# A hybrid decoder layer: how rows of tokens reach the experts, where norm weights are applied, and how roots are taken

## The chip, the core and the metric

The kernel runs on one core of a Trainium2 chip. A core has TensorE (PE in the profile; its weight loads are PEld), VectorE (DVE), ScalarE (ACT), GpSimd (POOL) and SyncE (SP), 16 DMA engines, SBUF and PSUM. Time is device microseconds of one launch; it is the median of several executions, and the profile is of one more.

## What is computed

One decoder layer on x of 1024 tokens by 1024 features, in float32. Cut to the parts that the change touches:

```python
def rms_norm(x, g):
    return x * rsqrt(mean(x * x, -1) + 1e-6) * g

h = rms_norm(x, attn_norm_g)
x = x + parallel_mixer(h)              # sparse and latent attention, both gated
x = x + memory_cross_attention(rms_norm(x, mem_x_norm_g), mem)
h = rms_norm(x, moe_norm_g)
x = x + hierarchical_moe(h)

def hierarchical_moe(h):               # 4 groups of 4 experts, top 2 in the best group
    for e in range(16):
        act = silu(h @ w_gate[e]) * (h @ w_up[e])        # 1024 -> 256
        y = y + combine[:, e] * (act @ w_down[e])        # 256 -> 1024
```

The mixer takes RMS norms of heads, too: of queries and keys of both attentions. Every one of them needs an inverse square root per token and head.

## The kernel before

**Stages.** `prep` norms x, projects it and builds keys and values (0 to about 145 us), scores the sparse attention's index, then runs gate projections (`gates`) on TensorE with two generators beside them: `queries`, which norms and rotates the queries of both attentions, and `topk`, which finds the 256th largest score of each row by 32 counting passes on VectorE and ACT (L1176, L1186). `attention` and the branch products follow, then `merge`: the output projection, memory attention and the router, pipelined by 128-token blocks through the class `Memory`; then `moe`. All products use a pair of float32r tiles, hi (ACT) and lo (the residue, on VectorE or GpSimd), and three matmuls (`mm3`, L522 to L524). The order of the instructions on each engine is set by a planner that simulates the program; the kernel adds only some orderings (`issue_after`).

**Roots.** `rsqrt` (L526 to L540) works on a tile of 128 rows and 1 to 17 columns: an add of eps (L533), a shift and a subtraction on the bits (L534, L535), and three Newton rounds of three instructions (L537 to L539), all on VectorE. It is called 15 times in the projections (11 columns), 12 times in `queries` (17), twice for the memory's keys (2 and 8), four times in `Memory.B` (8, without eps) and eight times in `Memory.F` (1).

**Norm weights of rows.** `Memory.E` adds the memory attention's output to x and sums squares; `F` (L465 to L477) takes the root, copies it to y (L469), scales x by y on ACT in two halves (L473) and multiplies by `moe_norm_g` on GpSimd in four pieces of 256 columns (L477), which also permutes each piece: feature 8i + c of a piece goes to place 32c + i. `G` finishes the router's logits; the class `Route` then ranks the experts in many small VectorE steps, and GpSimd scatters whole rows with their weights to a table in DRAM, `d_xs` (L197), sorted by expert. The permutation is made so that 32x32 transposes of the rows give the layout that the expert weights have, eight consecutive features per partition.

**Experts.** Each expert has a fixed room of rows (`ROOM`: 256, 256, 224, 224, 192, 192, 160, 160, five of 128, three of 96; 2592 in all). Big and small rooms alternate (`ORDER_`). The first 128 rows of experts 0 and 1 are read early, before the last rows are routed. `rows_of` reads n rows in four DMAs, one for each quarter of the features (L1646), as 1 KB packets into `xg` laid out in groups of 32 tokens; then the weights and token numbers, a few bytes per row (`emore`, L1652), which GpSimd turns into `ewt` and `etok` (L1654 to L1659). VectorE transposes each group (L1668) into `xT`, and ACT and VectorE split that into `eT` hi and lo (L1671, L1672). `gate_up` loads gate and up weights in halves of four chunks, 1 MB, into two buffers (`gu_raw`, L1689) and splits them (L1690 ACT, L1691 VectorE); `down` does so for the down weights (L1699, L1701 ACT, L1702 GpSimd). `first_big` and `first_small` make the activations, with rows or weights as the moving operand; `second` multiplies by the down weights, scales on ACT (L1722), and adds the result to the output in DRAM by an indirect DMA (L1708).

In the loop the first half of expert i+1's gate and up weights and then its rows are asked for just ahead of expert i's first product, the other half behind it. SyncE issues all loads in order; a load whose buffer is not free holds those behind it.

Of the kernel before, what the change touches and what calls it, by code (L numbers as in the profile page):

```python
# [267 lines left out]
class Memory:  # L268
# [196 lines left out]
    def F(u, t):  # L465

        K, nc = u.K, u.K.nc
        y = u.d['y', t] = u.ap.tile([128, 1], F32, name="my2", bufs=3)
        nc.vector.tensor_copy(y, K.rsqrt(u.d.pop(('ms2', t)), (128, 1)))  # L469
        for h in range(2):  # L470
            m = slice(h * 512, h * 512 + 512)
            xn = u.ap.tile([128, 512], F32, name="mxn", bufs=2)
            nc.scalar.activation(xn, u.x[:, t, m], AF.Copy, scale=y)  # L473
            for a in range(2):
                c, f = slice(a * 256, a * 256 + 256), slice(h * 512 + a * 256, h * 512 + a * 256 + 256)
                nat = lambda v: v.rearrange("p (i c) -> p i c", c=8)
                nc.gpsimd.tensor_mul(u.x[:, t, f].rearrange("p (c i) -> p i c", c=8), nat(xn[:, c]), nat(u.g_o[:, f]))  # L477
# [14 lines left out]
class Hybrid:  # L492
# [33 lines left out]
    def rsqrt(self, v, shape, eps=True):  # L526
        nc, n = self.nc, shape[-1]
        s = self.sm.tile([128, 17], I32, name="rq_s")
        y = self.sm.tile([128, 17], F32, name="rq_y")
        t = self.sm.tile([128, 17], F32, name="rq_t")  # L530
        s, y, t = s[:, :n], y[:, :n], t[:, :n]
# [98 lines left out]
    def consts(self):  # L630
# [5 lines left out]
        nc.vector.tensor_scalar(self.ident, jp, 0.0, None, op0=OP.is_equal)  # L636
        self.identb = ac.tile([128, 128], BF16, name="identb")
# [980 lines left out]
    def moe(self, route):  # L1618
# [20 lines left out]
        def rows_of(n, ex, exf, r, xg, xT, eT, early=False):  # L1639
# [3 lines left out]
            loads, last_load = [], None  # L1643
# [4 lines left out]
            more, wt, tok = (rt.tile([128, *sh], dt, name=nm, bufs=4) for nm, sh, dt in (("emore", (2, 4), F32), ("ewt", (2, 2), F32), ("etok", (2,), I32)))  # L1648
            for b in range(0, n, 128):
                m, b_ = min(128, n - b), b // 128  # L1650
                mo, w = more[0:m, b_], wt[0:m, b_]
                loads.append(nc.sync.dma_start(mo, table[at, r + b:r + b + m, D:D + 4].rearrange("o p f -> (o p) f")))  # L1652
# [7 lines left out]
            for q in loads:  # L1660
                for p in route.puts:
                    if early and p in route.late:
                        tc.declare_no_dep(q.ins, p.ins, reason="rows of a later block")
                    else:
                        tc.add_manual_dep(q.ins, p.ins.name, mybir.DependencyInfo(mybir.DependencyClass.Sync, mybir.DependencyReason.DATA), reason="rows of the table")
            with tc.issue_after(route.last_ix.ins) if early else nullcontext():
                for g in range(n // 32):
# [261 lines left out]
```

## Time and profile before

| What | us |
|---|---|
| median of 3 executions | 1431.34 (1428.15 to 1440.17) |
| the profiled execution's own time | 1433.15 |
| its span in the profile | 1431.3 |
| busy: PE, DVE, ACT, POOL | 1247.2, 976.1, 807.8, 550.6 |
| mean granted clock of TensorE | 0.937 |

The span runs from the first to the last instruction, so the execution has 1.85 us around it. Times in rows are counted from the start of the span. [...]

### The profile page before, as it was taken

Reading aid. Unit: us, or ns where it says so; the run is one execution under the profiler, and the core shown is the slowest. Engines: PE = TensorE matmul, PEld = TensorE weight load, DVE = VectorE, ACT = ScalarE, POOL = GpSimd, SP = SyncE. Lnnn points to the kernel's source line nnn. Section 1 sums busy time; section 2 is a strip of 40 time slices with the busy share of each in tenths; the row PEclk is TensorE's granted clock in tenths of the full one; section 3 lists DMA queues with packets and bytes.
Section 4 is the critical chain, followed back from the end, with each engine's and each line's share of the span. In section 5 each row is a group of like instructions: output and inputs, shape, how many; then the busy total and the mean of one; then the engine's idle time right before and its main releaser. Section 6 shows DMA issues by size and latency. Waiting matters only on the chain.

```text
span 1431.3 us, 20967 instructions
## 1 busy us (share of the span) xinstructions
PE 1247.2 (87%) x6684; PEld 1039.1 (73%) x6685; DVE 976.1 (68%) x2248; ACT 807.8 (56%) x1659; POOL 550.6 (38%) x676
## 2 busy tenths in 40 slices
PE   4779799998888999999998999999997478888993
PEld 4768688776666778888687787788986356777762
DVE  6785775989999757778887566232368977565660
ACT  5453554787663378888998421033454346556662
POOL 4575200425543111221343221211326555577673
PEclk9889899999999999999999999999997789999897
DMA  6555102535343454436321234621103679899973
GB/s 196 154 155 151 46 19 73 154 110 149 112 135 125 145 154 149 144 142 199 89 88 53 72 112 139 211 69 38 59 31 121 248 213 286 244 274 278 258 227 69
DMA packets 154154, 203.58 MB, mean 142 GB/s; under 512 B 70576, under 2 KB 102192, under 8 KB 154032
## 3 DMA queue, kind: packets, MB, share of 16 engines
q1 hardware_dynamic: 145440, 173.22, 39.6%
q0 software_dynamic: 7440, 24.71, 6.4%
q10 hardware_dynamic: 1152, 4.19, 0.7%
q8 instruction: 55, 0.90, 0.3%
q14 instruction: 67, 0.55, 0.1%
HBM read 134.61 MB, written 69.70 MB: 143 GB/s over the span
## 4 chain that ended last, share of the span: by engine, by line
PE 33%; DVE 22%; DMA 13%; ACT 10%; issue 8%; SPq 2%; POOL 2%; ACTq 0%; DVEq 0%; POOLq 0%
PE acc L522 3%; PE acc L523 3%; PE acc L524 3%; DMA xg<-d_xs 3%; PE s L522 2%; PE s L524 2%; PE s L523 2%; DVE ik_lo L1176 2%; DMA out_dram<-ey,etok 2%; DMA gu_raw<-in_moe_w_up_dram 2%; DVE ik_hi L1176 2%; PE s L919 2%; PE tp L1342 2%; DMA gu_raw<-in_moe_w_gate_dram 2%; DVE gu_lo L1691 1%
## 5 line engine op out<-in xcount | busy, mean ns | idle before, releaser
L514 POOL TENSOR_TENSOR wl<-wr,wh 128x512 fp32r<-128x512 f32 (+2 forms) x94 | 119.4, 1288 | 211.1 <-ACT wh L513 167.6
L510 DVE TENSOR_TENSOR PT_lo<-tp,PT_hi 128x512 fp32r<-128x512 f32 x152 | 102.0, 685 | 28.9 <-ACT PT_hi L509 27.4
L522 PE MATMUL s<-hT_hi,wh 128*128 128x512 f32 x256 | 102.5, 400 | 4.2 <-ACT s L1047 4.2
L1186 ACT ACTIVATE tk_junka<-sc,tk_b 128x512 bf16<-128x512 f32 (+2 forms) x96 | 79.4, 827 | 42.4 <-DVE tk_b L1183 27.3
L524 PE MATMUL s<-hT_hi,wl 128*128 128x512 f32 x256 | 101.5, 402 | 1.5 <-POOL wl L514 1.5
L523 PE MATMUL s<-hT_lo,wh 128*128 128x512 f32 x256 | 102.3, 400 | 0.0
L513 ACT ACTIVATE wh<-wr 128x512 fp32r<-128x512 f32 (+2 forms) x94 | 55.7, 610 | 82.2 <-PE acc L524 28.0
L509 ACT ACTIVATE PT_hi<-tp 128x512 fp32r<-128x512 f32 x152 | 86.9, 594 | 20.1 <-PE tp L1342 8.6
L522 PE MATMUL acc<-wh,hT_hi 128*128 128x512 f32 (+2 forms) x240 | 87.2, 365 | 8.8 <-ACT hT_hi L509 4.4
L1702 POOL TENSOR_TENSOR dn_lo<-dn_raw,dn_hi 128x1024 fp32r<-128x1024 f32 x32 | 83.2, 2625 | 16.7 <-ACT dn_hi L1701 16.4
L524 PE MATMUL acc<-wh,hT_lo 128*128 128x512 f32 (+2 forms) x240 | 88.5, 369 | 1.1 <-DVE hT_lo L510 1.1
L1691 DVE TENSOR_TENSOR gu_lo<-gu_raw,gu_hi 128x1024 fp32r<-128x1024 f32 x60 | 77.1, 1310 | 17.7 <-ACT gu_hi L1690 17.7
L523 PE MATMUL acc<-wl,hT_hi 128*128 128x512 f32 (+2 forms) x240 | 87.5, 364 | 0.9 <-POOL wl L514 0.9
L1690 ACT ACTIVATE gu_hi<-gu_raw 128x1024 fp32r<-128x1024 f32 x60 | 61.6, 1051 | 29.6 <-DMA gu_raw<-in_moe_w_gate_dram 20.9
L1324 DVE TENSOR_REDUCE low<-s 128x1 f32<-128x256 f32 (+3 forms) x64 | 49.0, 768 | 31.2 <-PE s L1323 31.0
L522 PE MATMUL s<-eT1h,gu_hi 128*128 128x224 f32 (+2 forms) x192 | 57.9, 302 | 13.8 <-DVE ea L1738 13.8
L1668 DVE STREAM_TRANSPOSE xT<-xg 128x256 f32<-128x256 f32 x73 | 25.9, 412 | 55.5 <-DMA xg<-d_xs 55.4
L522 PEld LDWEIGHTS s<-hT_hi,wh 128*128 128x128 f32 x256 | 49.3, 193 | 14.9 <-ACT s L1047 5.1
L522 PEld LDWEIGHTS acc<-wh,hT_hi 128*128 128x128 f32 x240 | 48.5, 202 | 15.5 <-ACT hT_hi L509 5.8
L524 PEld LDWEIGHTS s<-hT_hi,wl 128*128 128x128 f32 x256 | 49.4, 193 | 13.1 <-POOL wl L514 3.3
L928 DVE SCALAR_TENSOR_TENSOR sc<-rel,iw,sc 128x384 f32<-128x384 f32 (+5 forms) x42 | 41.9, 998 | 24.8 <-ACT rel L922 22.0
L523 PE MATMUL s<-eT1l,gu_hi 128*128 128x224 f32 (+2 forms) x192 | 57.9, 302 | 0.0
(533 smaller groups left out, 4255.0 us busy)
## 6 DMA issues: line engine op xcount, KB each, us to landing
d_xs<-zero SPq DMA_DIRECT2D x32, 516.0 KB, 3.8
dn_raw<-in_moe_w_down_dram SPq DMA_DIRECT2D x32, 512.0 KB, 5.8
gu_raw<-in_moe_w_gate_dram SPq DMA_DIRECT2D x30, 512.0 KB, 6.8
gu_raw<-in_moe_w_up_dram SPq DMA_DIRECT2D x30, 512.0 KB, 7.7
wr<-in_w_in_dram SPq DMA_DIRECT2D x48, 256.0 KB, 3.2
d_g<-s SPq DMA_DIRECT2D x32, 256.0 KB, 2.5
gt<-d_g SPq DMA_DIRECT2D x16, 512.0 KB, 3.9
dupq<-d_q SPq DMA_DIRECT2D x16, 256.0 KB, 3.9
```

The costliest lines, as they stand in the source:

```text
L509: self.nc.scalar.activation(hi, src, AF.Copy)
L510: self.nc.vector.tensor_sub(lo, src, hi.bitcast(F32))
L513: self.nc.scalar.activation(hi, src, AF.Copy)
L514: self.nc.gpsimd.tensor_sub(lo, src, hi.bitcast(F32))
L522: mm(out, a[0], b[0], start=start, stop=False)
L523: mm(out, a[0], b[1], start=False, stop=False)
L524: mm(out, a[1], b[0], start=False, stop=stop)
L1176: V.tensor_scalar(junks[0][:, :(t + 1) * 128], blk(t), b[:, i:i + 1].bitcast(F32), None, op0=op, op1=OP.add, accum_out=cnt[:, i:i + 1])
L1186: A.activation(junka[:, :(t + 1) * 128], blk(t), AF.Sign, bias=b[:, i:i + 1].bitcast(F32), accum_out=cnt[:, i:i + 1])
L1690: A.activation(hi[:, z], raw_z, AF.Copy)
L1691: E.tensor_sub(lo[:, z], raw_z, hi[:, z].bitcast(F32))
L1702: E.tensor_sub(lo, raw, hi.bitcast(F32))
```

## The change

Four edits. `F` scales into one tile of 1024 columns and multiplies by the norm weight once, on VectorE; the row is permuted as a whole, feature 8p + c to place 128c + p. `rsqrt` becomes an add of eps and a power of -0.5, both on GpSimd. Rows are loaded whole, one DMA per 128 rows (4 KB packets), by a function of its own that is called two experts ahead, with three `xg` buffers in the place of two and `xT`. `rows_of` transposes them on TensorE, eight 128x128 per 128 rows through the two PSUM tiles of `tp`, and splits from PSUM, per 128 rows. The weights of expert 2 are asked for ahead of the first late rows. A branch for overflowing experts, which does not run with these inputs, loses its copies.

```diff
 Memory.F
+        xn = u.ap.tile([128, D], F32, name="mxn", bufs=1)
         for h in range(2):
             m = slice(h * 512, h * 512 + 512)
-            xn = u.ap.tile([128, 512], F32, name="mxn", bufs=2)
-            nc.scalar.activation(xn, u.x[:, t, m], AF.Copy, scale=y)
-            for a in range(2):
-                c, f = slice(a * 256, a * 256 + 256), slice(h * 512 + a * 256, h * 512 + a * 256 + 256)
-                nat = lambda v: v.rearrange("p (i c) -> p i c", c=8)
-                nc.gpsimd.tensor_mul(u.x[:, t, f].rearrange("p (c i) -> p i c", c=8), nat(xn[:, c]), nat(u.g_o[:, f]))
+            nc.scalar.activation(xn[:, m], u.x[:, t, m], AF.Copy, scale=y)
+        nat = lambda v: v.rearrange("p (i c) -> p c i", c=8)
+        nc.vector.tensor_mul(u.x[:, t, 0:D].rearrange("p (c i) -> p c i", c=8), nat(xn), nat(u.g_o))
 rsqrt
         if eps:
-            nc.vector.tensor_scalar_add(v, v, EPS)
-        nc.vector.tensor_scalar(s, v.bitcast(I32), 1, None, op0=OP.logical_shift_right)
-        nc.vector.tensor_scalar(y.bitcast(I32), s, -1.0, float(0x5F3759DF), op0=OP.mult, op1=OP.add)
-        for _ in range(3):
-            nc.vector.tensor_mul(t, y, y)
-            nc.vector.scalar_tensor_tensor(t, t, -0.5, v, op0=OP.mult, op1=OP.mult)
-            nc.vector.scalar_tensor_tensor(y, t, 1.5, y, op0=OP.add, op1=OP.mult)
+            nc.gpsimd.tensor_scalar(v, v, EPS, None, op0=OP.add)
+        nc.gpsimd.tensor_tensor(y, v, self.mhalf.to_broadcast([128, n]), op=OP.pow)
 moe
-            xs = table[at, r:r + n, 0:D].rearrange("o (g i) (a f) -> (o a) i g f", i=32, a=4)
-            for a in range(4):
-                last_load = nc.sync.dma_start(xg[32 * a:32 * a + 32, 0:n // 32], xs[a])
+            for b in range(0, n, 128):
+                m = min(128, n - b)
+                last_load = nc.sync.dma_start(xg[0:m, b // 128], table[at, r + b:r + b + m, 0:D].rearrange("o p f -> (o p) f"))
...
-            with tc.issue_after(route.last_ix.ins) if early else nullcontext():
-                for g in range(n // 32):
-                    V.transpose(xT[:, :, g * 32:g * 32 + 32], xg[:, g].rearrange("p (c j) -> p c j", c=KD))
-            for k in range(0, KD, 4):
-                hi, lo, src = (h[:, k:k + 4] for h in (*eT, xT))
-                A.activation(hi, src, AF.Copy)
-                V.tensor_sub(lo, src, hi.bitcast(F32))
+            for b in range(0, n, 128):
+                m = min(128, n - b)
+                x = xg[0:m, b // 128].rearrange("p (c i) -> p c i", c=KD)
+                for k in range(0, KD, 4):
+                    p = self.tp().rearrange("p (c j) -> p c j", c=4)
+                    for c in range(4):
+                        nc.tensor.transpose(p[:, c, 0:m], x[:, k + c], self.ident[0:m, 0:m])
+                    self.split(*(h[:, k:k + 4, b:b + m] for h in eT), p[:, :, 0:m])
...
+        def load(k):
+            if k < NE:
+                n, r = (ROOM[k] - 128, 128) if k < 2 else (ROOM[ORDER_[k]], 0)
+                if k > 2:
+                    with tc.issue_after(loaded[k - 1][3].ins):
+                        expert.append(nc.values_load(nb[0:1, 16 + ORDER_[k]:17 + ORDER_[k]], engines=SP, min_val=0, max_val=NE - 1))
+                loaded[k] = rows_in(n, expert[k], r, xg3(xg_[k % 3]))
...
+        raws = [gate_up_in(2, expert[2], h) for h in range(2)]
+        load(0)
+        load(1)
...
         for i in range(2, NE):
-            n = ROOM[ORDER_[i]]
             if i + 1 < NE:
-                q = ORDER_[i + 1]
-                with tc.issue_after(load.ins):
-                    ex1 = nc.values_load(nb[0:1, 16 + q:17 + q], engines=SP, min_val=0, max_val=NE - 1)
-                gu1 = gate_up(i + 1, ex1, (0,))
-                hT1, load = tokens(i + 1, ROOM[q], ex1, route.ex[:, q:q + 1], 0)
+                load(i + 2)
+                gu1 = gate_up(i + 1, expert[i + 1], (0,))
+                n1, hT1 = tokens(i + 1)
             rest = (first_big if n > 128 else first_small)(n, gu, hT)
```

## Rows read from the trace of the kernel before

**Rows 1.** Windows: stretch, length, busy PE PEld DVE ACT POOL, clock, DMA share, GB/s
```profile
0.00:145.00 145.00, 109.89 (x544) 95.11 (x545) 100.33 (x300) 71.62 (x183) 83.03 (x153) 0.92 0.59 166
300.00:450.00 150.00, 135.53 (x597) 109.25 (x596) 146.28 (x427) 101.81 (x229) 68.10 (x66) 0.99 0.39 126
1045.00:1150.00 105.00, 70.17 (x425) 61.10 (x423) 88.81 (x380) 43.97 (x100) 55.27 (x86) 0.79 0.40 143
1150.00:1200.00 50.00, 40.17 (x152) 30.82 (x153) 33.53 (x71) 25.75 (x41) 23.40 (x44) 0.89 0.85 249
1200.00:1400.00 200.00, 178.47 (x993) 149.53 (x992) 117.04 (x174) 118.08 (x179) 142.29 (x128) 0.91 0.92 257
```

**Rows 2.** Chain that ended last: 300 to 450 by line; two pieces near 1088
```profile
by line: DVE ik_lo L1176 13.9%; DVE ik_hi L1176 13.6%; issue 11.1%; ACT tk_junka L1186 5.4%; DMA qraw<-d_raw 4.8%; DVE cnq L984 3.8%; DVE rq_t L538 3.6%; DVE qs L710 3.6%; DVE rq_t L537 3.3%; DVE tk_b L1183 3.1%; DVE ms L1011 3.0%; DVE rq_y
...
1087.43 1.55 DVE rq_t L537
1089.06 2.23 DVE rq_t L538
```

**Rows 3.** Windows of the instructions on tile rq_t: VectorE busy and count
```profile
0.00:145.00 145.00, 28.06 (x135) 0.92 0.59 166
300.00:450.00 150.00, 24.31 (x108) 0.99 0.39 126
1045.00:1150.00 105.00, 24.84 (x87) 0.79 0.40 143
```

**Rows 4.** GpSimd's multiply (busy, mean ns); timeline (start, length) at 1095 us
```profile
L477 POOL TENSOR_TENSOR xres<-mxn,g_o 128x256 f32<-128x256 f32 x32 | 22.6, 746 | 22.4 <-ACT mxn L473 19.8 <-DVE rq_y L535 2.5
...
1095.55 2.34 POOL L1702 TENSOR_TENSOR dn_lo<-dn_raw,dn_hi 128x1024 fp32r<-128x1024 f32 x1
...
1096.20 1.70 DVE L537 TENSOR_TENSOR rq_t<-rq_y 128x1 f32<-128x1 f32 x1
...
1098.50 0.15 DVE L539 SCALAR_TENSOR_TENSOR rq_y<-rq_t,rq_y 128x1 f32<-128x1 f32 x1
```

**Rows 5.** Small GpSimd operations: mean ns, and for L873 ns min, median, max
```profile
L1658 POOL TENSOR_TENSOR ewt<-ewt 128x1 f32<-128x1 f32 x2 | 0.3, 190 | 0.0
...
L873 POOL TENSOR_TENSOR kb<-kpe,rq_y x8: 616/641/1600, 68.1 to 142.2; 128x256 f32<-128x256 f32 x8
```

**Rows 6.** The residue of gate and up weights on VectorE: ns min, median, max
```profile
L1691 DVE TENSOR_TENSOR gu_lo<-gu_raw,gu_hi x60: 1184/1218/2847, 1134.0 to 1389.8; 128x1024 fp32r<-128x1024 f32 x60
```

**Rows 7.** Waits from 1160 to 1400 us: total, times, longest
```profile
DVE xT L1668 <- DMA xg<-d_xs: 55.4, 13, 8.2
...
SPq L1689 <- DVE gu_lo L1691: 43.7, 12, 7.5
...
ACT gu_hi L1690 <- DMA gu_raw<-in_moe_w_gate_dram: 20.6, 7, 7.7
...
PE s L522 <- DVE ea L1738: 13.8, 3, 5.3
```

**Rows 8.** Four TensorE transposes in the timeline (start, length)
```profile
1042.54 0.63 PE L359 MATMUL tp<-ident,xres 128*128 128x128 f32 x4
```

**Rows 9.** Windows, weights mostly, then rows; DMA issues: KB, us to landing
```profile
1253.00:1257.00 4.00, 4.00 (x33) 3.78 (x32) 1.28 (x4) 2.48 (x4) 1.04 (x3) 1.00 1.02 342
1245.00:1250.00 5.00, 5.00 (x24) 3.88 (x23) 2.50 (x5) 2.80 (x4) 2.01 (x2) 1.00 0.98 242
...
dn_raw<-in_moe_w_down_dram SPq DMA_DIRECT2D x32, 512.0 KB, 5.8
...
xg<-d_xs SPq DMA_DIRECT2D x28, 128.0 KB, 6.0
```

**Rows 10.** Windows of L1668, VectorE's transposes: busy and count
```profile
1200.00:1400.00 200.00, 19.56 (x55) 0.91 0.92 257
```

**Rows 11.** Entry to the experts: a piece of the chain, and TensorE's timeline
```profile
1183.78 8.82 DMA xg<-d_xs
...
1195.49 0.69 PE L1755 MATMUL tp<-ident,ea 128*128 128x128 f32 x2 [4.84 <-DVE ea L1749]
```

More of the change, by code (lines that the diff above doesn't have):

```diff
@@ L636, in consts @@
         nc.vector.tensor_scalar(self.ident, jp, 0.0, None, op0=OP.is_equal)
+        self.mhalf = cst.tile([128, 1], F32, name="mhalf")
+        nc.gpsimd.memset(self.mhalf, -0.5)
         self.identb = ac.tile([128, 128], BF16, name="identb")
@@ L1635, in moe, with rows_in, rows_of @@
         table = self.d_xs.rearrange("(e r) f -> e r f", e=NE)
-        def rows_of(n, ex, exf, r, xg, xT, eT, early=False):
+        def rows_in(n, ex, r, xg, early=False):
             at = slice(ex, ex + 1) if isinstance(ex, int) else ds(ex, 1)
-            loads, last_load = [], None
-            xs = table[at, r:r + n, 0:D].rearrange("o (g i) (a f) -> (o a) i g f", i=32, a=4)
-            for a in range(4):
-                last_load = nc.sync.dma_start(xg[32 * a:32 * a + 32, 0:n // 32], xs[a])
+            loads = []
+            for b in range(0, n, 128):
+                m = min(128, n - b)
+                last_load = nc.sync.dma_start(xg[0:m, b // 128], table[at, r + b:r + b + m, 0:D].rearrange("o p f -> (o p) f"))
                 loads.append(last_load)
-            more, wt, tok = (rt.tile([128, *sh], dt, name=nm, bufs=4) for nm, sh, dt in (("emore", (2, 4), F32), ("ewt", (2, 2), F32), ("etok", (2,), I32)))
+            more = rt.tile([128, 2, 4], F32, name="emore", bufs=4)
+            for b in range(0, n, 128):
+                m = min(128, n - b)
+                loads.append(nc.sync.dma_start(more[0:m, b // 128], table[at, r + b:r + b + m, D:D + 4].rearrange("o p f -> (o p) f")))
+            for q in loads:
+                for p in route.puts:
+                    if early and p in route.late:
+                        tc.declare_no_dep(q.ins, p.ins, reason="rows of a later block")
+                    else:
+                        tc.add_manual_dep(q.ins, p.ins.name, mybir.DependencyInfo(mybir.DependencyClass.Sync, mybir.DependencyReason.DATA), reason="rows of the table")
+            return n, xg, more, last_load
+        def rows_of(loaded, exf, eT, early=False):
+            n, xg, more, _ = loaded
+            wt, tok = (rt.tile([128, *sh], dt, name=nm, bufs=4) for nm, sh, dt in (("ewt", (2, 2), F32), ("etok", (2,), I32)))
             for b in range(0, n, 128):
@@ L1659, in rows_of @@
                     G.tensor_add(w[:, 0:1], w[:, 0:1], mo[:, 1:2])
[L1660 to L1665, printed above, removed]
-            with tc.issue_after(route.last_ix.ins) if early else nullcontext():
-                for g in range(n // 32):
-                    V.transpose(xT[:, :, g * 32:g * 32 + 32], xg[:, g].rearrange("p (c j) -> p c j", c=KD))
@@ L1675, in weights, with gate_up_in @@
+            return *eT, wt, tok
         def weights(nm, ex, pat, **kw):
             return I[nm][0, slice(ex, ex + 1) if isinstance(ex, int) else ds(ex, 1)].rearrange("o " + pat, **kw)
-        def gate_up(m, ex, halves, E=V):
+        def gate_up_in(m, ex, h):
+            if m:
+                raw = r2.tile([128, 2, 4, 256], F32, name="gu_raw", bufs=2)
+                raw = [raw[:, z] for z in range(2)]
+            else:
+                raw = [ra.tile([128, D], F32, name="dn_raw", bufs=2).rearrange("p (c f) -> p c f", c=4) for _ in range(2)]
+            for raw_z, nm in zip(raw, ('moe_w_gate', 'moe_w_up')):
+                nc.sync.dma_start(raw_z, weights(nm, ex, "(p c) f -> p (o c) f", c=8)[:, 4 * h:4 * h + 4, :])
+            return raw
@@ L1788, in moe @@
         nb = route.places(r3)
-        h, load = tokens(0, nA, 0, 0.0, 128)
+        raws = [gate_up_in(2, expert[2], h) for h in range(2)]
+        load(0)
+        load(1)
+        nA, h = tokens(0)
         last = (128, rest(), dn, *hA[2:])
@@ L1793, in moe @@
         hA = h
-        h, load = tokens(1, nB, lead[0], route.le[:, 0:1], 128)
+        load(2)
+        nB, h = tokens(1)
         last = (128, rest(), dn1, *hB[2:])
@@ L1799, in moe @@
         last = (nA, rest(), dn, *hA[2:])
-        ex = lead[1]
-        gu = gate_up(2, ex, (0,))
-        hT, load = tokens(0, ROOM[ORDER_[2]], ex, route.ex[:, 15:16], 0)
+        load(3)
+        gu = gate_up(2, expert[2], (0,), V, raws)
+        n, hT = tokens(2)
         rest = first_small(nB, gu1, hB)
-        gu = gu + gate_up(2, ex, (1,), V)
+        gu = gu + gate_up(2, expert[2], (1,), V, raws)
         second(*last)
```

51 lines of the change are left out of this document (21 added, 30 removed).

## Prediction

> **What bounds the kernel now.** The windows by stage come first. Outside five stretches TensorE is near full and this change adds nothing there; the five are [rows 1]: the projections with their norms (0 to 145 us), the queries with the top-k search (300 to 450), the end of memory attention with the router (1045 to 1150), the entry to the experts (1150 to 1200) and the experts (1200 to 1400). In 300 to 450 VectorE is busy 146.28 of 150 us; in 1045 to 1150 it is busy 88.81 of 105 while TensorE is granted 0.79 of its clock, so partly at its lower level; in 1200 to 1400 TensorE (178.47 of 200, at 0.91) and the DMA engines (0.92) are both nearly full.
>
> Next the chain that ended last. In 300 to 450 its two largest lines are the counting steps of the top-k search on VectorE, and the Newton lines L537 and L538 stand among its first nine [rows 2]. In the memory stage the chain runs through single Newton steps of one column that took 1.55 and 2.23 us [rows 2]. Why so long, the timeline shows: beside a 2.34 us GpSimd subtraction a 128x1 step took 1.70 us; with nothing beside it, 0.15 [rows 4].
>
> Last, the waits among the experts [rows 7]: VectorE stood 55.4 us before its 32x32 transposes, for rows of tokens. It takes its work in order, so the residues of the weights (gu_lo) stood behind them, and SyncE then waited 43.7 us for gu_lo before it could refill a weight buffer.
>
> **The roots.** A root is 12 VectorE instructions (11 without eps); the nine that touch rq_t are busy 28.06, 24.31 and 24.84 us in the three VectorE stretches [rows 3]. Three more per call at 0.15 [rows 4] to 0.17 us make about 36, 30 and 29 us that leave VectorE. GpSimd gains two per call. Its add costs the 0.19 us of a 128x1 operation [rows 5]. The trace has no power. From below it is another 0.19. Above, a software power might do some 40 multiply-like steps; at the 2.4 ns per column of a GpSimd multiply (616 ns for 256 columns [rows 5]) that is 0.1 us per column, 1.1 us for 11 and 1.7 for 17 columns. [...] I take 0.1, which rests on the nearest multiply, and keep the rest for a rival. Latency then hardly changes: 12 links of 0.2 us were 2.4 us, two GpSimd instructions and a crossing are 1 to 2.2. What is new is the queue: the power stands behind GpSimd's splits and multiplies, and what reads the root (cn, xn, y) holds everything behind it on VectorE.
>
> Queries: VectorE falls to 146 - 30 = 116 of 150, so TensorE becomes the bound. It idled 150 - 135.5 = 14.5 us [rows 1], which caps the gain. Waits on weights and loads stay in that; I take -6 (bounds -14 and +4). Projections: TensorE idled 145 - 110 = 35 us, about 10 of them before the first row can arrive; of the other 25 I take a fifth, -5 (-12 to +2).
>
> **The norm weights.** Thirty-two strided GpSimd multiplies of 746 ns, 22.6 us in all [rows 4], go; eight 128x1024 VectorE multiplies come. The nearest is gu_lo, same size, both inputs in SBUF, 1.218 us in the median [rows 6]: 8 x 1.22 = 9.8 us. Between 1045 and 1150 VectorE goes from 88.8 to 88.8 - 29 + 9.8 = 70, and some 6 us less as steps that are not Newton's stop being stretched by those multiplies: 64, against TensorE's 70.17 x 0.79 = 55 us at full clock [rows 1]. If VectorE alone set the pace, the stretch would shorten by 25. ACT's scaling, the hop to GpSimd for the root and the scatters on GpSimd's queue stay in each token block's chain, so I take two thirds, -17 (-25 to -2). Once x no longer waits on GpSimd's multiplies, the scatter's issues there are next to be late.
>
> The new multiply reads both inputs with a step of 32 bytes. The row: GpSimd's strided multiply took 746 ns [rows 4] against 641 in the median for an equal unit-stride one [rows 5], 16% more; no run shows VectorE on such a step. [...]
>
> **The rows of tokens.** Issues on SyncE fall from four DMAs per load to one per 128 rows, and packets grow from 1 KB to 4 KB. While rows were loading, the queues moved 242 GB/s; with weights almost alone, 342 [rows 9]; 128 KB of rows took 6.0 us to land, 512 KB of weights 5.8 [rows 9]. Fifty-five groups of 32 rows fall in 1200 to 1400 [rows 10], 7.2 MB: 29.8 us at the one rate, 21.1 at the other. The DMA floor goes from 0.92 x 200 = 184 to 175.
>
> [...]
>
> VectorE loses 19.56 us of transposes in that stretch [rows 10]; its residues no longer wait behind them, as rows come two experts ahead. TensorE gains eight transposes per block of up to 128 tokens, 24 blocks, 192 in all. Four took 0.63 us [rows 8], at most 0.16 each: 30 us, of which 55/81, some 20 us, fall in 1200 to 1400. TensorE's floor goes from 178.47 x 0.91 = 162 to 182 us. So it takes over from the DMA: before, 200 us ran 16 above the higher floor (184); with half of that excess the stretch takes 190, -10. ACT and VectorE split from PSUM in 48 pieces instead of 36; the time VectorE gave up hides it. At the entry the second load of rows landed 8.82 us after its issue and TensorE stood 4.84 us [rows 11]; both first loads now go out together, -4. Together -14 (-25 to +7).
>
> **Sum.** -5 - 6 - 17 - 14 = -42. The profiled execution took 1433.15 us (span 1431.3), 1.8 above the median of 1431.34: 1433 - 42 = 1391, or 1389 from the median. Forecast 1390.
>
> **Rivals.** (1) The power is long, GpSimd the pace; the slower side. In the queries GpSimd is busy 68.1 us over 12 calls, 5.7 of each 12.5 [rows 1]: room for 6.8 us, 0.40 per column of 17. In the projections 83.0 over 15, 5.5 of 9.7: room for 0.38 per column of 11. Beyond, 0.1 us per column costs 20 and 17 us. With about -24 left from the other parts it decides from 0.46 us per column; at 0.65 the time is 1433 - 24 + 51 + 45 = 1505. For it: no row shows a power. Against: even 40 steps stay at a quarter of that.
>
> (2) TensorE inherits ACT's waits. PSUM has two tiles for transposes, and their split stands behind gu_hi on ACT, which waited 20.6 us for gate weights [rows 7]. If all of it falls on TensorE, the experts give +7 instead of -14: 1412. Against: TensorE lost only 13.8 us to its largest wait there [rows 7], so its order has slack.
>
> (3) VectorE was full without being the pace: the chain names it only because it is never idle, and TensorE's work is what ends each stretch. Then projections and queries give nothing and the memory stage -8: 1411. For it: TensorE's own waits in these stretches are short.
>
> **How the numbers follow.** Forecast 0.62, rival 1 0.11, rival 2 0.13, rival 3 0.14. The forecast's own bounds add up to -76 (1357) and +11; both at once is unlikely. The range 1358 to 1430 holds it and rivals 2 and 3, and leaves rival 1 out above. One per cent, 14 us, is about what a measurement of this kernel tells from no change: faster than 1417 is 0.60 of the forecast's 0.62 with 0.07 and 0.09 from rivals 2 and 3, 0.76; slower than 1446 is rival 1, 0.11; the rest, 0.13, is within.
>
> **What would show it.** Right: VectorE under 125 of 150 us in the stretch of the queries; a POOL power under 2 us for 17 columns; the router's last scatter 10 to 25 us closer to the end of the output projection than now; no VectorE wait for rows; TensorE above 0.95 of its clock among the experts; the stretch from first expert to last shorter by 10 to 15 us. Wrong: POOL the busiest engine before 450 us with VectorE waiting for roots (rival 1); TensorE waiting for the split of a transposed block behind gu_hi (rival 2); less VectorE time and the same start of attention (rival 3). A VectorE multiply of 2 us or more would take a third of the memory stage's term.

## The result and the profile after

The changed kernel takes 1421.65 us in the median of 9 runs (1419.37 to 1427.02), the kernel before 1431.53 beside it: ratio 0.9911, 95% interval 0.9885 to 0.9936. It is 10 us faster where 41 were forecast: the right direction and inside the range, but a quarter of the size. The profiled execution took 1426.21 us (span 1424.4). One of the ten executions of e2 below took 6603 us, over four times the others, and is left out of its ratio.

Four instructions cut both kernels into the same stages: the first softmax of attention (first start), the output projection's last addition to x, the last scatter of routed rows and the last scatter of results (last starts). The views of these lines follow, first of the kernel before, then of the changed one; the columns are count, duration min/median/max in ns, first and last start in us.

```profile
L1326 ACT ACTIVATE P<-s,low x64: 465/738/1121, 508.6 to 658.9; 128x256 f32<-128x256 f32 x16, 128x384 f32<-128x384 f32 x8, 128x512 f32<-128x512 f32 x8, 128x640 f32<-128x640 f32 x8
L1605 DVE TENSOR_TENSOR xres<-acc,xres x16: 659/692/694, 913.8 to 1026.7; 128x512 f32<-128x512 f32 x16
L197 POOL DMA_INDIRECT d_xs<-xres,ix x16: 952/972/2000, 1102.1 to 1151.9; - x16
L1708 POOL DMA_INDIRECT out_dram<-ey,etok x24: 1345/1625/2445, 1173.2 to 1419.0; - x24
```

```profile
L1318 ACT ACTIVATE P<-s,low x64: 464/738/1116, 495.2 to 647.0; 128x256 f32<-128x256 f32 x16, 128x384 f32<-128x384 f32 x8, 128x512 f32<-128x512 f32 x8, 128x640 f32<-128x640 f32 x8
L1597 DVE TENSOR_TENSOR xres<-acc,xres x16: 679/692/694, 901.5 to 1018.1; 128x512 f32<-128x512 f32 x16
L197 POOL DMA_INDIRECT d_xs<-xres,ix x16: 952/1027/2555, 1093.1 to 1142.8; - x16
L1716 POOL DMA_INDIRECT out_dram<-ey,etok x24: 1353/1596/2418, 1170.6 to 1412.3; - x24
```

Attention starts 508.6 - 495.2 = 13.4 us earlier, the output projection ends 8.6 earlier, the routed rows go out 9.1 and the last result 6.7 earlier. A second profile of the same changed kernel (e14 below) gives 12.3, 11.7, 11.8 and 11.5. So the gain is made before attention. Between attention and the end of the output projection, where the change touches nothing, the two profiles of one kernel differ by 4 us. Behind it the memory stage (to the last scatter of routed rows) gains 0.1 to 0.5 us where 17 were forecast, and the experts lose 0.3 to 2.4 where 14 were to be gained.

The windows of the changed kernel, same columns as [rows 1]:

```profile
0.00:145.00 145.00, 108.41 (x544) 91.49 (x545) 62.76 (x120) 71.66 (x183) 118.28 (x184) 0.95 0.59 167
300.00:450.00 150.00, 136.01 (x595) 112.94 (x594) 143.07 (x299) 99.35 (x223) 111.79 (x93) 0.94 0.41 132
1045.00:1150.00 105.00, 66.11 (x416) 57.45 (x415) 83.27 (x284) 43.57 (x91) 48.98 (x81) 0.85 0.46 170
1150.00:1200.00 50.00, 41.55 (x190) 32.32 (x188) 21.78 (x31) 26.05 (x43) 20.36 (x32) 0.93 0.83 260
1200.00:1400.00 200.00, 183.30 (x1120) 153.14 (x1121) 97.62 (x127) 118.37 (x188) 115.63 (x128) 0.94 0.81 241
```

In the projections VectorE gave up 38 us and TensorE is as busy as before. In the queries VectorE is still full: 143 of 150, not under 125. Among the experts the DMA engines fell from 0.92 to 0.81, VectorE from 117 to 98, and TensorE rose to 183 of 200.

What the new instructions cost (groups of the changed kernel by shape, count | busy us, mean ns; then the norm multiply's own line and TensorE's transposes of rows):

```profile
L529 POOL TENSOR_TENSOR rq_y<-ms,mhalf 128x17 f32<-128x17 f32 x12 | 37.4, 3121 | 0.2
L529 POOL TENSOR_TENSOR rq_y<-ms,mhalf 128x11 f32<-128x11 f32 x15 | 32.1, 2141 | 0.4
L529 POOL TENSOR_TENSOR rq_y<-mms,mhalf 128x1 f32<-128x1 f32 x8 | 4.5, 568 | 0.6
...
L475 DVE TENSOR_TENSOR xres<-mxn,g_o x8: 1983/2037/3116, 1047.0 to 1123.6; 128x1024 f32<-128x1024 f32 x8
...
L1673 PE MATMUL tp<-ident,xg 128*128 128x128 f32 (+3 forms) x176 | 25.4, 270 | 8.8 <-DMA emore<-d_xs 4.5 <-DVE eT1l L508 3.6 <-issue 0.6
```

A power costs 568 ns for one column and 160 more for each further one ((3121 - 568) / 16); 100 were assumed. The norm multiply takes 2.04 us, not 1.22. The transposes are priced rightly: 25.4 us for 176 (the other 16, of the early rows, stand in rows of their own).

The largest waits among the experts, 1160 to 1400 us (total us, times, longest):

```profile
DVE gu_lo L1699 <- ACT gu_hi L1698: 65.1, 26, 9.8
POOL out_dram L1716 <- ACT ey L1730: 46.4, 8, 10.6
ACT gu_hi L1698 <- DMA gu_raw<-in_moe_w_gate_dram: 21.5, 6, 6.2
POOL dn_lo L1710 <- ACT dn_hi L1709: 19.3, 10, 2.7
POOL etok L1661 <- DMA out_dram<-ey,etok: 18.8, 5, 6.3
```

VectorE's 55.4 us for rows [rows 7] are gone, as forecast. In their place it waits 65.1 us for ScalarE's high parts (17.7 before), and GpSimd waits 46.4 us for results to scatter (5.1 before), with the down weights' residues queued behind.

### The profile page after: what moved, and what is told of

It reads as the page before. It is cut to its first block, busy times and chain, and to the rows that moved or that the text cites. A ratio compares the mean times of both kernels' runs of the same rounds, so it can differ in the third digit from the quotient of the medians.

```text
span 1424.4 us, 20689 instructions
## 1 busy us (share of the span) xinstructions
PE 1249.4 (88%) x6876; PEld 1043.0 (73%) x6877; DVE 887.7 (62%) x1699; ACT 808.0 (57%) x1671; POOL 596.9 (42%) x723
## 4 chain that ended last, share of the span: by engine, by line
PE 48%; DVE 14%; DMA 10%; ACT 10%; issue 8%; POOL 6%; SPq 0%; ACTq 0%; POOLq 0%; DVEq 0%
PE acc L520 6%; PE acc L521 6%; PE acc L522 6%; PE s L520 4%; PE s L522 4%; PE s L521 4%; DMA dn_raw<-in_moe_w_down_dram 2%; DMA gu_raw<-in_moe_w_up_dram 2%; ACT tk_junka L1178 2%; PE tp L1334 2%; PE s L911 2%; PE tp L1431 1%; PE s L1414 1%; DMA out_dram<-ey,etok 1%; DMA gu_raw<-in_moe_w_gate_dram 1%
## 5 line engine op out<-in xcount | busy, mean ns | idle before, releaser
L1699 DVE TENSOR_TENSOR gu_lo<-gu_raw,gu_hi 128x1024 fp32r<-128x1024 f32 x60 | 80.6, 1365 | 71.0 <-ACT gu_hi L1698 69.0
L529 POOL TENSOR_TENSOR rq_y<-ms,mhalf 128x11 f32<-128x11 f32 (+3 forms) x29 | 71.8, 2482 | 0.7
L1716 POOL DMA_INDIRECT out_dram<-ey,etok x24 | 40.3, 1681 | 63.9 <-ACT ey L1730 47.2
L520 PEld LDWEIGHTS s<-hT_hi,wh 128*128 128x128 f32 x256 | 49.3, 193 | 13.8 <-ACT s L1039 4.2
L521 PEld LDWEIGHTS s<-hT_lo,wh 128*128 128x128 f32 x256 | 49.4, 193 | 10.1
L920 DVE SCALAR_TENSOR_TENSOR sc<-rel,iw,sc 128x384 f32<-128x384 f32 (+5 forms) x42 | 42.2, 1004 | 22.5 <-ACT rel L914 19.3
L520 PE MATMUL s<-eT1h,gu_hi 128*128 128x224 f32 (+2 forms) x192 | 54.3, 283 | 1.8 <-ACT eT1h L507 1.8
```

Of the source, the lines that this page charges most:

```text
L520: mm(out, a[0], b[0], start=start, stop=False)
L521: mm(out, a[0], b[1], start=False, stop=False)
L529: nc.gpsimd.tensor_tensor(y, v, self.mhalf.to_broadcast([128, n]), op=OP.pow)
L1699: E.tensor_sub(lo[:, z], raw_z, hi[:, z].bitcast(F32))
```

## The experiments

All are compared with the kernel before run beside them (ratios); the times of the stages, in us, come from one profile each. "Memory" is from the end of the output projection to the last scatter of routed rows, the measure that the prediction named; "landing" from that scatter's issue to the first load of rows; "experts" from that scatter to the last scatter of results; "loop" the part of it from the first scatter of results on. Where kernels share the code of a stage, the memory column agrees within about 2 us. The others do less well: the fourteen profiles with the power in the projections and queries start attention between 490.9 and 496.6 (e12 is not one of them), and the experts of e1 and e2, which are those of the kernel before, take 7 us longer than its own. So only patterns over several rows are read.

| kernel | ratio (95% interval) | attention at | memory | landing | experts | loop |
|---|---|---|---|---|---|---|
| before | 1 | 508.6 | 125.2 | 9.2 | 267.1 | 245.8 |
| changed | 0.9911 (0.9885 to 0.9936) | 495.2 | 124.7 | 12.6 | 269.5 | 241.7 |
| e14, the same again | 0.9901 (0.9866 to 0.9935) | 496.3 | 125.1 | 12.6 | 267.4 | 239.1 |
| e1 roots alone | 0.9924 (0.9888 to 0.9960) | 493.9 | 119.2 | 8.8 | 274.7 | 249.5 |
| e2 norm alone | 1.0078 (1.0042 to 1.0114) | 507.1 | 128.0 | 8.6 | 273.9 | 249.3 |
| e3 rows alone | 0.9978 (0.9947 to 1.0010) | 507.5 | 124.6 | 12.5 | 267.2 | 239.0 |
| e4 lead weights late | 0.9857 (0.9793 to 0.9921) | 494.8 | 120.1 | 13.0 | 274.1 | 241.2 |
| e5 half the transposes | 0.9883 (0.9834 to 0.9932) | 496.6 | 124.1 | 12.8 | 266.7 | 239.3 |
| e6 transposes twice | 0.9972 (0.9947 to 0.9997) | 493.4 | 124.3 | 10.6 | 276.5 | 251.7 |
| e7 down residues on VectorE | 0.9887 (0.9828 to 0.9946) | 495.1 | 124.6 | 12.8 | 263.6 | 235.0 |
| e8 norm on GpSimd | 0.9878 (0.9821 to 0.9935) | 492.7 | 120.0 | 11.8 | 265.3 | 237.9 |
| e9 third weights late | 0.9862 (0.9788 to 0.9936) | 495.6 | 124.8 | 7.6 | 263.0 | 240.5 |
| e12 Newton in projections | 0.9913 (0.9880 to 0.9947) | 498.4 | 124.4 | 12.6 | 271.1 | 242.6 |
| e13 rows one ahead | 0.9903 (0.9870 to 0.9936) | 492.3 | 125.5 | 12.8 | 269.4 | 240.8 |
| e16 norm at unit stride | 0.9895 (0.9856 to 0.9934) | 491.2 | 121.1 | 12.4 | 269.8 | 241.0 |
| e10 = e7 + e8 | 0.9830 (0.9746 to 0.9913) | 490.9 | 118.1 | 12.4 | 265.0 | 237.1 |
| e11 = e7 + e8 + e9 | 0.9780 (0.9704 to 0.9855) | 493.6 | 118.2 | 8.5 | 259.3 | 235.6 |
| e17 = e7 + e9, norm reordered on ScalarE | 0.9816 (0.9785 to 0.9847) | 493.6 | 121.0 | 7.9 | 262.2 | 237.3 |

**The three parts alone.** e1 takes only the new root into the kernel before, e2 only the norm multiply on VectorE (in four blocks of 256, the old order of features), e3 only the rows; e3 is the changed kernel with the other two parts undone; it scales the second half of a row after the first multiplies have overwritten part of it, so its rows differ from the reference's.

```diff
+        nat = lambda v: v.rearrange("p (a i c) -> p a c i", a=4, c=8)
+        nc.vector.tensor_mul(u.x[:, t, 0:D].rearrange("p (a c i) -> p a c i", a=4, c=8), nat(xn), nat(u.g_o))
```

These are e2's new lines in F; e1 and e3 take theirs from the diff of the change.

> The kernel before with the roots alone taken by a power on GpSimd; the norm weights stay on GpSimd, the rows as they were. Theory A (the roots pay in the queries and nowhere else): attention starts 12 to 14 us earlier than before, as in the changed kernel, and in the memory stage the power, which now shares GpSimd with the four multiplies per token block, gives nothing or takes some back; ratio 0.988 to 0.995. Rival (the roots also pay in the memory stage, and it is the norm weight on VectorE that spoils it there): attention 13 us earlier and the router's last scatter 20 us or more earlier; ratio 0.985 or less.

> The kernel before with the norm weights alone moved to VectorE (one multiply of 128x1024 per token block, the same layout in four blocks of 256); roots by Newton on VectorE, rows as they were. Theory A (VectorE paces the memory stage, so 8 multiplies of 2.04 us = 16 us on it cost more than the GpSimd multiplies did): the router's last scatter comes 0 to 8 us later than before; ratio 1.000 to 1.006. Rival (GpSimd's multiplies and their stretching of VectorE's small steps were the pace): the last scatter comes 4 us or more earlier; ratio 0.997 or less.

> The changed kernel with the roots back to Newton on VectorE and the norm weights back on GpSimd (in the layout of whole rows): the change of the rows alone. Theory A (the rows' change moves the wait of the experts to other places and gives nothing): from the router's last scatter to the last scatter of results about 270 us, as in both kernels; ratio 0.997 to 1.003. Rival (the rows' change pays, and what is lost is lost by the other two parts in the memory stage): the experts 5 us or more shorter; ratio 0.996 or less.

The roots alone give 11 us (0.76%): attention starts 14.7 us earlier, the memory stage is 6.0 shorter, and the experts, whose code is the old one, are 7.6 longer. The norm weight on VectorE alone loses 11 (0.78%), 2.8 of them in the memory stage; its experts grew by 7, too. Why isn't settled. The rows alone give nothing that can be measured in the total. Theory A holds for the rows and, but for the 6 us of the memory stage, for the roots; the norm cost more than it allowed. The three ratios add up to 0.998 where the change has 0.991: the parts don't simply add, though the difference is barely clear of the intervals. That VectorE does not pace the memory stage shows in its last 112 us, before and in e1 (columns of [rows 1]):

```profile
1040.00:1152.00 112.00, 76.92 (x461) 66.72 (x462) 94.53 (x395) 46.13 (x104) 56.66 (x88) 0.80 0.39 139
...
1024.00:1136.00 112.00, 74.66 (x518) 65.45 (x517) 81.06 (x279) 52.00 (x116) 72.96 (x108) 0.87 0.42 148
```

With Newton gone VectorE has 31 us free in the same length of time, and TensorE has 37. No engine is full. Over the whole stage VectorE's busy time falls from 99.4 us to 84.9, and of these 14.5 us 6 come off its length. That the blocks' chains of dependent steps set the length is inferred from this, not shown.

**The norm multiply.** e8 puts it back on GpSimd in the changed kernel (four multiplies of 256, after both scalings). e16 leaves the reordering out:

```diff
-        nc.vector.tensor_mul(u.x[:, t, 0:D].rearrange("p (c i) -> p c i", c=8), nat(xn), nat(u.g_o))
+        nc.vector.tensor_mul(u.x[:, t, 0:D], xn, u.g_o)
```

> The changed kernel with the norm weights back on GpSimd (four multiplies of 128x256 per token block, after both halves are scaled); roots by the power and the rows' change stay. Theory D (the norm weight on VectorE, 8 times 2.04 us in the middle of the router's steps, took back what the roots gave in the memory stage; the power alone put the last scatter at 1136.2 us, the changed kernel has 1142.8): last scatter at 1134 to 1139 us; by theory C the end follows by as much, if the entry to the experts does not hold it: ratio 0.985 to 0.989. Rival (the norm weight is not what holds the scatter): 1141 us or later, ratio 0.990 to 0.993.

> The changed kernel with VectorE's norm multiply at unit stride on all three operands; the reordering of the features is left out, so the experts see features in another order than the reference. Theory D1 (the 32-byte step of the two inputs is the cost): the multiply takes 1.2 to 1.3 us, as the residue of equal size did, and the memory stage (first transposes of x to last scatter, 200.2 us in the changed kernel) loses 3 to 6 us. Rival D2 (1024 columns of three f32 operands cost 2 us there whatever the step, as beside GpSimd's work): 1.8 us or more, and no change of the stage.

The multiply's line in e16, against the changed kernel's 1983/2037/3116:

```profile
L475 DVE TENSOR_TENSOR xres<-mxn,g_o x8: 1212/1218/2287, 1042.8 to 1115.3; 128x1024 f32<-128x1024 f32 x8
```

D1 holds: the 32-byte step of the two inputs takes 2.04 - 1.22 = 0.82 us, two thirds on top. The forecast's row for GpSimd, 746 ns against 641 [rows 4, 5], does not bear on it: that multiply read both inputs in order and wrote with a step of 128 bytes, and the 641 are of one that repeats a few values over its columns.

In the memory stage, four groups stand apart. The eight profiles with the multiply and the order of the change (changed, e5, e6, e7, e9, e12, e13, e14) take 124.1 to 125.5 us, as long as Newton did with the multiply on GpSimd (before, e3: 125.2, 124.6). With the power and the multiply on GpSimd (e1, e8, e10, e11) the stage takes 118.1 to 120.0, with the multiply at unit stride on VectorE (e16, e17) 121.1 and 121.0. e4 (120.1) has another edit in this stage and is read below. Theory D holds for the stage: e8 is 4.7 to 5.1 us shorter; the rest of its 10 us earlier last scatter (1132.8) arose ahead of the stage. But even at 1.22 us, the price of the forecast, the stage is some 4 us shorter than before, not 17.

**What ends the memory stage, and the entry to the experts.** The chain of waits of the changed kernel there (start, length in us):

```profile
1123.97 9.92 DMA gu_raw<-in_moe_w_up_dram
1133.91 1.06 ACT gu_hi L1698
1135.00 1.23 DVE gu_lo L1699
...
1138.90 0.95 POOL d_xs L197
...
1142.81 12.37 DMA d_xs<-xres,ix
1155.39 0.34 SPq L1638
1155.78 3.48 DMA emore<-d_xs
```

The leading expert's weights come by DMA; their residues, four from 1128.6 to 1136.2 us, stand in VectorE's queue ahead of the router's last steps, which wait with them until the last index step at 1138.45. Then the last scatter takes 12.4 us to land, and the first load of rows goes out behind it, at 1155.39. In the 20 us before, the DMA engines are full (shares of 0.96 and 1.01), and TensorE, busy 0.21 and 2.69 us of 10, is granted 0.57 and 0.50 of its clock:

```profile
1120.00:1130.00 10.00, 0.21 (x2) 0.13 (x2) 7.43 (x43) 2.61 (x5) 6.13 (x7) 0.57 0.96 308
1130.00:1140.00 10.00, 2.69 (x12) 2.17 (x11) 7.42 (x33) 4.27 (x5) 2.51 (x34) 0.50 1.01 404
```

The same 0.50 is the lower level that the prediction speaks of: in the kernel before, TensorE is granted 1.00 from 1045 to 1085 us and 0.50 from 1131 to 1151.

e4 (the first two lines) orders VectorE's residues behind the last index step; e9 (the rest) moves the third expert's first weights behind the first rows.

```diff
+        with tc.issue_after(route.last_ix.ins):
+            gu1 = gate_up(1, lead[0], (0,), V) + gate_up(1, lead[0], (1,), V)
...
-        raws = [gate_up_in(2, expert[2], h) for h in range(2)]
         load(0)
         load(1)
+        raws = [gate_up_in(2, expert[2], h) for h in range(2)]
```

> The changed kernel with one order added: VectorE's four residues of the leading expert's weights go behind the router's last index step instead of ahead of it. In the changed kernel they wait for weights from 1126 to 1136 us, and the last index step stands behind them until 1138.45. Theory B (these weights are the end of the memory stage now): the last index step comes 6 to 9 us earlier, the last scatter too, and the kernel gains 4 to 9 us against the changed one (1421.65): ratio to the kernel before 0.985 to 0.989. Rival (the scatters and the first rows are held by something else, such as the weights then in the queues): the index earlier, the end within 2 us of the changed kernel, ratio 0.990 to 0.992.

> The changed kernel with the 2 MB of gate and up weights of the third expert issued behind the first two loads of rows instead of ahead of them. In the changed kernel these four transfers go out at 1140.2 to 1142.1 us beside the router's last scatter, which then takes 12.37 us from issue to landing (9.2 in the kernel before), and the first rows wait for it. Theory E (these weights hold the scatter): the scatter lands in 6 to 9 us, the first rows go out 3 to 6 us after less; what of it reaches the end depends on whether the weights, now later by some 12 us, are missed: by theory E the end 2 to 4 us earlier, ratio to the kernel before 0.987 to 0.990. Rival (the transfers at the entry are simply full, and what is not moved then is moved later): the first results earlier, the third expert later, end within 2 us of the changed kernel or later, ratio 0.990 to 0.996.

In e4 the last index step comes 6.8 us earlier and the last scatter 4.6, but the first result at 1171.1 (1170.6 in the changed kernel) and the last at the same 1412.3: the chain to the first result now runs through a load of down weights that takes 16.0 us. In the trace the rival is right about the end; the ratio, though 0.9857, has an interval that holds both theories, and its median of 1422.35 us is the changed kernel's. In e9 the landing falls to 7.6 us and the experts to 263.0. The pattern holds over all kernels: with these weights ahead of the rows the landing is 10.6 to 13.0 us (twelve profiles), without them 7.6 to 9.2 (before, e1, e2, e9, e11, e17). That is 3 to 5 us that the change put there itself. From the last scatter of rows to the first result (experts less loop) the kernels before, e1 and e2 take 21.3 to 25.2 us, the changed kernel 27.8 and e14 28.3, e9 22.5; e11 takes 23.7 where e10 took 27.9. Theory E holds for the scatter; what of it reaches the kernel's time is not clear of the intervals.

**The experts.** e5 (first change) transposes only the first half of a block and splits it twice; e6 (second) transposes each slice twice; e7 (third) makes the loop's down residues on VectorE; e13 (fourth) loads rows one expert ahead, and leaves out the `load(3)` ahead of the loop.

```diff
+                    if k == 0:
                         p = self.tp().rearrange("p (c j) -> p c j", c=4)
...
-                    for c in range(4):
-                        nc.tensor.transpose(p[:, c, 0:m], x[:, k + c], self.ident[0:m, 0:m])
+                    for c in range(8):
+                        nc.tensor.transpose(p[:, c % 4, 0:m], x[:, k + c % 4], self.ident[0:m, 0:m])
...
-            dn = down(i, expert[i])
+            dn = down(i, expert[i], V)
...
-                load(i + 2)
+                if i + 1 not in loaded:
+                    load(i + 1)
```

> The changed kernel with half of TensorE's transposes of token rows left out: the second four slices of a block are split from the first four's PSUM tile, so the rows that the experts see are not the reference's; splits, loads and everything else stay. Theory C (TensorE paces the experts after the change: it was busy 183 of 200 us there, 25 us of it in these transposes): TensorE loses 12.7 us and the last scatter of results comes 8 to 12 us closer to the router's last scatter (269.5 us in the changed kernel); ratio to the kernel before 0.983 to 0.986. Rival (the loop of weight buffers paces them: residue, refill, landing, residue): 3 us or less; ratio 0.989 to 0.993.

> The changed kernel with each of TensorE's transposes of token rows done twice into the same place: 25 us more on TensorE among the experts, nothing else. Theory C (TensorE is the pace): the experts grow by 18 to 25 us; ratio to the kernel before 1.003 to 1.010. Rival (the loop of weight buffers): TensorE's idle 17 us take up most, the experts grow by less than 10 us; ratio below 0.998.

> The changed kernel with the residues of the down weights of the experts in the loop made by VectorE (28 at some 1.22 us) and not by GpSimd (2.4 us each, behind the scatters of results and the token numbers that wait for them). Rival of theory C (the loop of weight buffers paces the experts, and GpSimd's queue is the late part of it: the chain names GpSimd's residue with 6.7 per cent and the down weights' transfer with 10.6): the experts get 5 to 12 us shorter; ratio to the kernel before 0.982 to 0.988. Theory C (TensorE): 3 us or less; ratio 0.989 to 0.993.

> The changed kernel with the rows of the experts in the loop loaded one expert ahead and not two. Theory C' (after the change neither the rows nor their landing hold the experts: TensorE with its transposes, GpSimd's queue and the full transfers at the entry do): the same within 3 us, 0.997 to 1.003 of e14. Rival (two ahead is what took VectorE's 55.4 us of waits for rows away): TensorE's transposes wait for rows, 5 to 15 us later.

TensorE's transposes in e6 and e5 (the changed kernel's row stands above):

```profile
L1673 PE MATMUL tp<-ident,xg 128*128 128x128 f32 (+3 forms) x352 | 43.1, 268 | 5.7 <-DVE eT1l L508 4.2 <-DMA emore<-d_xs 1.3
...
L1674 PE MATMUL tp<-ident,xg 128*128 128x128 f32 (+3 forms) x88 | 12.3, 259 | 1.3 <-DMA emore<-d_xs 1.3
```

17.7 us more on TensorE (not 25) lengthen the experts by 7 to 9 us and the kernel by 9 to 10 (0.9972 against 0.9911 and 0.9901); 13.1 less shorten them by 1 to 3, which is not clear of noise. The rival's numbers hold in both. The loop says more: nine kernels with the changed kernel's products and residues (changed, e3, e4, e8, e9, e12, e13, e14, e16) take 237.9 to 242.6 us there, e6 takes 251.7 and e5 239.3. Of TensorE time that is added some six tenths reach the end of the loop, of what is taken away nothing that can be told. So TensorE is close to being the pace without being it. e7 finds another part: its experts are 4 to 6 us shorter and GpSimd's busy time falls from 115.6 to 62.2 of 200:

```profile
1200.00:1400.00 200.00, 180.65 (x1115) 151.19 (x1113) 111.94 (x149) 118.28 (x187) 62.15 (x93) 0.94 0.79 236
```

GpSimd's queue was late: the residues stood behind scatters that waited for results. The scatters wait on in e7 (62.9 us for results, 46.4 in the changed kernel), but nothing that the weights need stands behind them. The four kernels with this edit (e7, e10, e11, e17) have loops of 235.0 to 237.3 us, below all nine without it; beside e8, though, it gives only 0.8 (e10). e13 shows no gain of loading two experts ahead over one: ratios 0.9903 and 0.9901, each good to about 5 us, and loops of 240.8 and 239.1.

The loop also shows what the totals hide. With the old rows it takes 245.8, 249.5 and 249.3 us (before, e1, e2), with the new ones 240.4 in the mean of the nine: the rows' change does shorten it, by 5 us against the kernel before and by 8 against the mean of the three. The longer way from the last scatter to the first result takes this back.

**The projections.** e12 keeps the old function beside the new one, for the 15 roots of 11 columns.

```diff
-            y = self.rsqrt(ms(i)[:, 0:11], (128, 11))
+            y = self.rsqrt_newton(ms(i)[:, 0:11], (128, 11))
```

> The changed kernel with the 15 roots of 11 columns in the projections back to Newton on VectorE; the power stays in the queries and the memory stage. The prediction's term of the projections was -5 us; in the changed kernel the last of the projections' evictions starts at 160.6 us against 160.1 before, with VectorE standing 13.8 us for roots. Theory F (the power's 2.15 us for 11 columns, on a GpSimd busy 118 of 145 us, is as late as Newton was, the term is nil): attention starts within 2 us of the changed kernel's 495.2, ratio 0.989 to 0.993. Rival (the term is there, hidden by something else): attention 4 us or more later, ratio 0.994 or more.

Attention starts at 498.4, 2 to 3 us later than in the two profiles of the changed kernel and 1.8 to 7.5 later than in all fourteen with the power; the output projection ends at 1016.2, inside the 1010.2 to 1018.1 of the fourteen, and the ratio is the changed kernel's. Whether the forecast's -5 exists there stays open; nothing of it is seen in the total.

**The same again, and together.** e14 is the changed kernel; e10 joins e7 and e8, e11 adds e9. e17 joins e7 and e9 and lets ScalarE's scaling write the features in the rows' order, with g_o reordered once.

```diff
+        nat = u.x[:, t, 0:D].rearrange("p (i c) -> p c i", c=8)
         for h in range(2):
+            nc.scalar.activation(xn[:, h * 512:h * 512 + 512].rearrange("p (c i) -> p c i", c=4), nat[:, 4 * h:4 * h + 4], AF.Copy, scale=y)
+        nc.vector.tensor_mul(u.x[:, t, 0:D], xn, u.g_o)
```

> The changed kernel, unchanged, run beside e13, e16 and e17 for the differences to them: 0.989 to 0.993 of the kernel before.

> The changed kernel with the norm weights on GpSimd and the residues of the loop's down weights on VectorE, the two edits that each gave about 4 us alone (0.9878 and 0.9887 against 0.9911). If they act in different stages (memory stage, experts) they add: ratio 0.984 to 0.987. If each only shifts the order of the experts, they don't: 0.987 to 0.990.

> The same with the third expert's first weights behind the first rows as well. Theory E: 2 to 4 us better than without, ratio 0.981 to 0.985. Rival (full transfers at the entry): the same as without, or worse.

> The changed kernel with three edits: ScalarE's scaling of x writes the features in the order of the rows (it reads them with the 32-byte step), so that VectorE's norm multiply is at unit stride and right; the loop's down residues on VectorE; the third expert's first weights behind the first rows. By D1 and theories C' and E it is 12 to 18 us faster than the changed kernel: 0.978 to 0.983 of the kernel before, level with the version that multiplies on GpSimd (0.978). If ScalarE's strided read doubles its 0.72 us, 16 times 0.7 us come back in the chain of each block: 0.983 to 0.988.

e10 is at 0.983, as if its two edits added; but its gain over e8 is in the memory stage (118.1 against 120.0) and ahead of it, not in the experts (265.0 against 265.3), so that they act in different stages isn't shown. e11 at 0.978 (median 1406.54 us, 3 under e10's) and e17 at 0.982 (1409.78, in the range expected) beat both kernels: their intervals lie below the changed kernel's, where those of the single edits overlap it. Which of the two is better isn't settled. In e17 the 32-byte step shows on ScalarE too: a scaling of 512 columns takes 1270 ns in place of 717 in the mean.

## Why the prediction was right or wrong, step by step

**Projections and queries, -11 forecast, -12 to -13 measured** at attention's start. The sum was right, the reason not, so the match is luck. "TensorE becomes the bound" in the queries failed: VectorE stayed full. The last counting step of the search, in both kernels:

```profile
L1176 DVE TENSOR_SCALAR_CACHE_REDUCE ik_hi<-sc,tk_b x51: 598/1141/1278, 234.8 to 453.2; 128x1024 bf16<-128x1024 f32 x17, 128x896 bf16<-128x896 f32 x16, 128x384 bf16<-128x384 f32 x16, 128x512 bf16<-128x512 f32 x1
```

```profile
L1168 DVE TENSOR_SCALAR_CACHE_REDUCE ik_hi<-sc,tk_b x51: 599/1142/1277, 232.9 to 435.3; 128x1024 bf16<-128x1024 f32 x17, 128x896 bf16<-128x896 f32 x16, 128x384 bf16<-128x384 f32 x16, 128x512 bf16<-128x512 f32 x1
```

It starts 17.9 us earlier: VectorE was the pace, so more than half of the 30 us that left it [rows 3] came off, and 13 us reached attention. "VectorE under 125 of 150" was a wrong sign to look for: where the pace-setting engine loses work the stretch gets shorter, and the engine stays full. In the projections e12 leaves the 5 us open; a power of 2.14 us is about as long a link as the forecast's 12 Newton links of 0.2.

**Rival 1, the long power.** Mis-sized but harmless: 3.12 us for 17 columns, 0.18 per column, against 0.1 assumed (an estimate, by a count of 40 steps that no run shows) and 0.46 from which it would decide. GpSimd rose to 112 of 150 in the queries and did not become the pace there. In the projections, with 118 of 145, it is the busiest engine and VectorE stands 13.8 us for its roots, so the sign named for this rival did show there; whether that took the 5 us stays open with e12.

**The memory stage, -17 forecast, -0.1 to -0.5 measured** from the end of the output projection to the last scatter (125.2 us before, 124.7 and 125.1 after). The sign named for it, 10 to 25 us, did not come. The step that failed is "if VectorE alone set the pace, the stretch would shorten by 25 ... I take two thirds". VectorE was busy there without being the pace. Its busy time in the stage falls from 99.4 us to 84.9 in e1 and, with the multiply at the forecast's own price, to 83.2 in e16, not by 25; and of these 14.5 and 16.2 us only 6 and 4 come off the stage. That is rival 3's reasoning, in the stage where it was given 8 us. The multiply at 2.04 us instead of 1.22 takes back what is left: the forecast had 2 us or more down as a third of the stage's term, some 6 us; by e16 and e17 against the eight profiles it costs 3 to 4.5. The lead weights' residues in front of the router's last steps hold another 5 (e4), which the forecast had no term for.

**The experts, -14 forecast, +0.3 to +2.4 measured.** The waits of VectorE for rows were real and went. The forecast's two parts fared differently. The loop, -10 forecast ("with half of that excess the stretch takes 190"), gave 4 to 7 us against the kernel before: the right direction, mis-sized. TensorE's transposes, priced as a floor, cost nothing that e5 can tell from noise, and the wait that is next late was not named: GpSimd's queue of scatters and residues, some 4 us by the loops with e7's edit. The entry, forecast -4, is the step that failed: from the last scatter of rows to the first result it became 6.5 to 7 us longer than before (2.6 to 3.7 longer than in e1 and e2). "Both first loads now go out together" overlooked that the same edit sends 2 MB of weights ahead of them, beside the scatter they wait for; e9 takes 5 to 6 us of it off again. Rival 2, TensorE behind ScalarE, did not come in its form: TensorE waits 3.6 us for the split of a transposed block, and ScalarE 10.5 for TensorE's transposes. The DMA floor fell further than forecast: e3, which moves rows the new way and as many bytes in the 200 us (256 against 257 GB/s), has a share of 0.83 in place of 0.92, 166 us in place of 184, where 175 were forecast (the changed kernel: 0.81 at 241 GB/s). It bought no shorter waits for weights: ScalarE waited 21.5 us for gate weights, 20.6 before.

## What to carry to other kernels

An engine that is busy in nearly every slice need not be the pace: remove work from it alone, as e1 did, before pricing a stage by its sum. When a prefetch is hoisted, list what it is hoisted past and what that waits for; here the weights went ahead of rows whose scatter they then slowed. Put a layout change on the engine that has room: e8's four multiplies took GpSimd 3.1 us per block where VectorE's one took 2.04, and the stage was 5 us shorter. And cut a stage where its code begins: measured from attention on, 4 us of difference between two profiles of one kernel would hide what the memory stage did.

## What the runs showed of the hardware that was not expected

Reading f32 with a step of 32 bytes made a multiply of 1024 columns on VectorE 2.04 us in place of 1.22 (the changed kernel and e16), and ScalarE's scaling of 512 columns 1.27 in place of 0.72 (e17 and the changed kernel). A power on GpSimd took 0.57, 2.14 and 3.12 us for 1, 11 and 17 columns, so about 0.41 us and 0.16 per column. From the issue of the last indirect scatter of 128 rows to the first load of rows it took 7.6 us, or 12.6 where 2 MB of weights had been asked for in the 2.6 us before it (e9 and the changed kernel).
